# A hybrid diffusion step on one core: z/dt projection first, output projection's first columns inside the ordered region, second shift off TensorE

## The chip, the cores and the metric

The kernel runs on one core of a Trainium2 chip. The time is that of one execution on the device in microseconds (us); the figure for a kernel is the median of its runs. TensorE does matrix products and transposes, VectorE (DVE) and ScalarE (ACT) do elementwise work, GpSimd (POOL) does elementwise work and issues DMAs, and SyncE (SP) issues the large weight loads. Each engine works through one queue in a fixed order.

## The reference

One layer of a model with 128 context tokens and 256 latent tokens (384 together), width 2048, all in fp32:

```python
sh1, sc1, g1, sh2, sc2, g2 = split(silu(cond) @ w_mod + b_mod, 6)   # cond: c or c_ctx, 2 rows
h = x * (1 + sc1) + sh1
q, k, v, u, gt, z, xbc, dt = split(h @ w_in)
o_a = attention(q, k, v, cached keys and values, bias)              # 16 heads, A
o_b = silu(layer_norm(dwconv31(u * sigmoid(gt))))                   # B
xbc = silu(dwconv5(xbc)); dt = softplus(dt + dt_bias)
o_c = rms_norm((ssd_forward + ssd_backward + d * xs) * silu(z))     # C, chunks of 128
mix = concat(o_a, o_b, o_c) @ w_out                                 # 2048 x 2048
x = layer_norm(ALPHA * x + g1 * mix)
h = x * (1 + sc2) + sh2
x = layer_norm(ALPHA * x + g2 * ffn(h))                             # 5632 wide, dwconv3, SwiGLU
```

## The kernel before, in words

**Precision.** Most fp32 products are done as three passes: a matrix is split into a high part (rounded by ScalarE, line 226, tile `whi`) and a low part (the difference, by VectorE, line 227, tile `wlo`), and high x high, high x low and low x high are summed in PSUM. A weight piece of 512 KB is loaded by SyncE into one of four `raw` buffers, split as two halves, and used by TensorE; `whi` and `wlo` have eight half-piece buffers each. The products with tokens in PSUM's partitions (`tok_mm`, lines 444 to 446) have 512 columns (264 in the z/dt projection), those with channels there (`chan_mm`, lines 450 to 452) have 384.

**Stages.** First sc1, sh1, h, and the u, gt and xbc columns of `h @ w_in` with the first half of v. Then an *ordered region* (lines 871 to 890), in which TensorE's instructions stand in the order in which the program writes them: the other half of v (`phase_v`), q and k of head pair 0, the z/dt projection (`phase_zd`), q and k of pairs 1 to 7. Then the output projection (`wo`) in column groups of 512, 512, 512, 256 and 256, with gate, residual and LayerNorm statistics behind each (`mix_evac`), LayerNorm (`ln1`), and the FFN, which is the rest of the kernel.

**What sets the order around the change.** Beside the main projections a small planner (`_Flow`) keeps generators with due times: after each few matmuls `flow.tick` moves its clock on and runs what is due. The generators are: transposes of xbc (`tok_gen`), the state-space scan (`ssm_gen`, which waits for `dt_gen`), attention (`attn_gen`; pairs 5 to 7 wait until the scan is through), the LayerNorm of branch B, and `mod2_gen`, which computes g1, sc2 and sh2 with cond as a 32-column weight (line 762; 32 loads of 512 KB into three `v` buffers for each of the three, in sets of three pieces). A second list (`flow.bg`) holds the 124 taps of the 31-wide convolution for VectorE (lines 351 and 355) and hands them out at `flow.rate` of the time that ticks. When the projections are written, `flow.drain` writes whatever is left, with no projection between. Outside the region, and on all other engines everywhere, a list scheduler sets the order by its own estimate of times and by priority; weight loads and splits have a high one (`HP`).

Inside the FFN the second gate g2 is already computed without TensorE: `g2_piece` loads rows of `w_mod` into a `raw` buffer and VectorE multiplies them by cond (spread over the partitions by a DMA) and sums along the row (line 820, 128 x 512, the sum into `macc`).

The order of `wo`'s rows is `ORDER`: branch B (8 to 11), heads 0 to 3, branch C (12 to 15), heads 4 to 7.

Of the kernel before, what the change touches and what calls it, by code (L numbers as in the profile page):

```python
# [14 lines left out]
D = 2048  # L15
KC = 16
# [31 lines left out]
class _Flow:  # L48
# [29 lines left out]

    def drain(self):
        while self.bg:  # L80
            self.bg.pop(0)[0]()
        while self.q:
            self.now = max(self.now, self.q[0][0])
            self.run()
# [12 lines left out]
def _build(tc, ctx, a):  # L97
# [264 lines left out]
    def conv_ln_gen():  # L362
# [21 lines left out]
        for i in range(4):  # L384
# [5 lines left out]
            cat[8 + i] = c  # L390
        yield 2.7, 0.0
# [211 lines left out]
    def ssm_gen():  # L603
# [10 lines left out]
        ready.add("ssm")  # L614

# [116 lines left out]
    def attn_gen():  # L732
        for hp in range(8):
# [35 lines left out]
    def mod2_end(g):  # L769
# [17 lines left out]
        dst, bias = (s2, b2p) if g == 1 else (h2b, P_("bsh2", 0, 16))  # L787
        V.tensor_tensor(out=dst.rearrange("p (j b) c -> p j b c", j=4), in0=pv,
                        in1=bc(bias.rearrange("p (j b) -> p j b", j=4), 3, 2), op=ALU.add)
        yield 0.5, 1.0  # L790

    def mod2_gen(most, gap):
        i = 0
        while i < 96:
# [28 lines left out]
    def g2_piece(i):  # L823
# [47 lines left out]
    with tc.manual_schedule(engines={mybir.EngineType.PE}):  # L871
        for i in range(8):
            do_conv5(i)
        for i in range(4):
            flow.bg += conv31_steps(i)
        flow.rate = 0.4
        flow.add(30.0, tok_gen())
        flow.add(0.0, mod2_gen(3, 8.0))
        flow.add(40.0, conv_ln_gen())
# [75 lines left out]
    def mix_evac(t, cg, c0, n, ps, gb):  # L955
        rr = r[t][cg][:, c0:c0 + n]
        tmp = g_t(512)
        with tc.high_priority(offset=HP):
            V.tensor_tensor(out=tmp[:, :n], in0=ps[:, :n], in1=gb[t > 0][:, c0:c0 + n], op=ALU.mult)
        V.scalar_tensor_tensor(out=rr, in0=rr, scalar=ALPHA, in1=tmp[:, :n], op0=ALU.mult, op1=ALU.add)  # L960
        V.bn_stats(out=st1[t][:, cg + c0 // 256, :], in_=rr)

    for cg in range(4):
        gb = [gate(0, s, cg) for s in range(2)]
        for t in range(3):
            if cg % 2 == 0:
                rt[t][cg // 2] = vt_t() if cg == 0 else (ckv_t, ckv_t, v_t)[t]()
            r[t][cg] = rt[t][cg // 2][:, cg % 2, :]
            G.dma_start(out=r[t][cg], in_=a["xtok"][128 * t:128 * t + 128, 512 * cg:512 * cg + 512])
        n = 512 if cg < 3 else 256  # L970
        npk = 1024 // n
        ps = [ps_t() for _ in range(3)]
        for kk in range(KC // npk):
            hi, lo = wpiece(a["wo"][:, KC * 512 * cg + kk * 1024:KC * 512 * cg + (kk + 1) * 1024], 1024)
# [282 lines left out]
```

## Time and profile before

| what | us |
|---|---|
| median of 3 runs (lowest, highest) | 1859.7 (1859.32, 1862.12) |
| the profiled execution's own time | 1860.49 |
| its span in the trace | 1858.6 |
| TensorE busy | 1814.3 |
| VectorE busy | 1144.0 |
| ScalarE busy | 779.7 |
| GpSimd busy | 57.3 |

The profile comes from the one profiled execution, whose time is 1.9 us above its span and 0.8 us above the median. Matmuls are pipelined, so the distance from one start to the next is what one costs; the printed duration of one is longer. [...] A timeline gives instructions in order of time, with the idle time ahead of one and what ended it in brackets.

### The profile page before, as it was taken

The numbers are of one execution on the slowest core, as the hardware profiler recorded it, in microseconds if no ns is written. First come the engines' busy times: TensorE is split into PE (matmuls) and PEld (weight loads), VectorE is DVE, ScalarE is ACT, GpSimd is POOL, SyncE is SP. The second block draws the span as 40 slices with busy tenths as digits, with TensorE's granted clock in tenths as the row PEclk, the third lists the DMA queues.
The fourth block names the chain that finished last, engine by engine and source line by source line (L and its number), as shares of the span: only waits on it lengthen the run. The fifth ranks groups of instructions, "written<-read, shape, count | busy, mean of one in ns | idle before, by whom it ended". The sixth has DMA issues, their size and how long they took to land. (4 is left out here: it accounts for less than half of the span.)

```text
span 1858.6 us, 29014 instructions
## 1 busy us (share of the span) xinstructions
PE 1814.3 (98%) x11054; PEld 1634.8 (88%) x11054; DVE 1144.0 (62%) x2329; ACT 779.7 (42%) x1479; POOL 57.3 (3%) x141
## 2 busy tenths in 40 slices
PE   8999999999987999999999999999999999999998
PEld 6888978887854889999988999988999988999987
DVE  3865899457552448566733667644667644666577
ACT  4222544465555336444433444422444423444424
POOL 0000000110101000000000000000000000000000
PEclk9999999999987999999999999999999999999999
DMA  8999477776755543444444454444444444444454
GB/s 314 308 323 318 142 258 250 268 272 227 243 191 175 170 140 122 136 143 136 159 125 131 159 171 161 141 127 142 161 163 159 147 125 142 147 159 158 119 152 139
DMA packets 108011, 335.67 MB, mean 181 GB/s; under 512 B 12456, under 2 KB 17032, under 8 KB 107872
## 3 DMA queue, kind: packets, MB, share of 16 engines
q1 hardware_dynamic: 101280, 311.65, 50.9%
q0 software_dynamic: 6592, 22.18, 4.0%
q8 instruction: 86, 1.41, 0.3%
q14 instruction: 53, 0.43, 0.1%
HBM read 328.98 MB, written 4.79 MB: 180 GB/s over the span
## 5 line engine op out<-in xcount | busy, mean ns | idle before, releaser
L226 ACT CAST whi<-raw 128x512 fp32r<-128x512 f32 (+1 forms) x755 | 467.9, 621 | 908.7 <-PE mm L451 320.5
L227 DVE TENSOR_TENSOR wlo<-raw,whi 128x512 fp32r<-128x512 f32 (+1 forms) x755 | 521.1, 691 | 488.3 <-ACT whi L226 484.8
L450 PE MATMUL mm<-hl,whi 128*128 128x384 f32 x1245 | 427.0, 343 | 1.4 <-ACT whi L226 1.1
L451 PE MATMUL mm<-hl,whi 128*128 128x384 f32 x1245 | 420.1, 337 | 0.0
L452 PE MATMUL mm<-hl,wlo 128*128 128x384 f32 x1245 | 419.3, 337 | 0.0
L450 PEld LDWEIGHTS mm<-hl,whi 128*128 128x128 f32 x1245 | 233.8, 188 | 13.4 <-issue 6.7
L451 PEld LDWEIGHTS mm<-hl,whi 128*128 128x128 f32 x1245 | 234.1, 188 | 0.9 <-DVE hl L243 0.4
L452 PEld LDWEIGHTS mm<-hl,wlo 128*128 128x128 f32 x1245 | 234.0, 188 | 0.0
L450 PE MATMUL sc<-hl,whi 128*128 128x384 f32 x659 | 222.8, 338 | 0.0
L451 PE MATMUL sc<-hl,whi 128*128 128x384 f32 x659 | 221.8, 337 | 0.0
L452 PE MATMUL sc<-hl,wlo 128*128 128x384 f32 x659 | 221.7, 336 | 0.0
L450 PEld LDWEIGHTS sc<-hl,whi 128*128 128x128 f32 x659 | 123.6, 188 | 2.9 <-ACT whi L226 1.6
L451 PEld LDWEIGHTS sc<-hl,whi 128*128 128x128 f32 x659 | 123.7, 188 | 0.0
L452 PEld LDWEIGHTS sc<-hl,wlo 128*128 128x128 f32 x659 | 123.7, 188 | 0.0
L820 DVE SCALAR_TENSOR_TENSOR junk<-raw,gb 128x512 bf16<-128x512 f32 x128 | 87.9, 686 | 47.5 <-DMA raw<-wg 47.4
L444 PE MATMUL mm<-whi,hl 128*128 128x512 f32 (+2 forms) x261 | 92.5, 355 | 1.0 <-ACT m L437 0.8
L446 PE MATMUL mm<-whi,hl 128*128 128x512 f32 (+2 forms) x261 | 90.8, 348 | 0.0
L444 PE MATMUL mm<-whi,t 128*128 128x512 f32 (+1 forms) x232 | 90.6, 390 | 0.0
L445 PE MATMUL mm<-wlo,hl 128*128 128x512 f32 (+2 forms) x261 | 90.5, 347 | 0.0
L445 PE MATMUL mm<-wlo,t 128*128 128x512 f32 (+1 forms) x232 | 90.5, 390 | 0.0
L446 PE MATMUL mm<-whi,t 128*128 128x512 f32 (+1 forms) x232 | 90.4, 390 | 0.0
L355 DVE SCALAR_TENSOR_TENSOR t<-g,par,t 128x399 f32<-128x399 f32 x120 | 73.4, 630 | 1.3
(337 smaller groups left out, 2458.4 us busy)
## 6 DMA issues: line engine op xcount, KB each, us to landing
raw<-wu SPq DMA_DIRECT2D x176, 512.0 KB, 3.7
v<-wm SPq DMA_DIRECT2D x96, 512.0 KB, 5.4
raw<-wd SPq DMA_DIRECT2D x79, 512.0 KB, 3.6
m<-wm SPq DMA_DIRECT2D x128, 256.0 KB, 5.6
raw<-wA SPq DMA_DIRECT2D x32, 512.0 KB, 5.4
raw<-wqk SPq DMA_DIRECT2D x32, 512.0 KB, 4.4
raw<-wo SPq DMA_DIRECT2D x32, 512.0 KB, 3.6
raw<-wg SPq DMA_DIRECT2D x32, 512.0 KB, 3.6
```

Source lines behind the costliest of these rows:

```text
L226: S.copy(out=hi[:, :w], in_=rw)
L227: V.tensor_tensor(out=lo[:, :w], in0=rw, in1=hi[:, :w].bitcast(F32), op=ALU.subtract)
L355: V.scalar_tensor_tensor(out=cvo[i][:, :399], in0=glu[i][:, j:j + 399], scalar=P_("conv_w", 31 * i + j), in1=cvo[i][:, :399], op0=ALU.mult ...
L444: PE.matmul(ps[:, :n], A, hi[:, w0:w0 + n], start=k == 0, stop=False)
L445: PE.matmul(ps[:, :n], A, lo[:, w0:w0 + n], start=False, stop=False)
L446: PE.matmul(ps[:, :n], B, hi[:, w0:w0 + n], start=False, stop=k == last)
L450: PE.matmul(ps[:, :T], A, hh[k], start=k == k0, stop=False)
L451: PE.matmul(ps[:, :T], A, hl[k], start=False, stop=False)
L452: PE.matmul(ps[:, :T], B, hh[k], start=False, stop=k == k1)
L820: V.scalar_tensor_tensor(out=j, in0=w, scalar=1.0, in1=cbc[s], op0=ALU.mult, op1=ALU.mult, accum_out=macc[:, 16 * s + kt, kq:kq + 1])
```

## The change

1. `phase_zd` and `dt_gen` come first in the region, then `phase_v`, then q and k of all eight pairs. The taps are handed out at 0.7 in place of 0.4, `mod2_gen` has a gap of 11.5 us in place of 8.0, and the scan and attention start with due times of 30 and 50 us.
2. The first 512 columns of `wo` move into the region, behind the last q and k and ahead of the drain (`wo_group`, `cat_split`). Rows whose input isn't there yet make the planner run its generators until it is (`flow.advance`).
3. sh2 no longer goes through `mod2_gen` (64 pieces in place of 96). It is computed as g2 is, with its own array `wsh2`: odd pieces by VectorE (`dve_gemv`), even ones by a GpSimd product into an `m` tile and a ScalarE sum over it (`pool_gemv`). From the end of the scan one piece is written every 9 us; from the second group of `wo` on, one behind each weight piece.

```diff
-        while i < 96:
+        while i < 64:
...
+    def pool_gemv(w, kt, kq):
+        for s in range(2):
+            j = m_t()
+            G.tensor_tensor(out=j, in0=w, in1=cbc[s], op=ALU.mult)
+            S.activation(out=j, in_=j, func=AF.Copy, accum_out=macc[:, 16 * s + kt, kq:kq + 1])
+
+    def sh2_piece():
+        i = sh2_done[0]
+        if i == 32:
+            return
+        sh2_done[0] += 1
+        kq, pr = i // 8, i % 8
+        if pr == 0:
+            cond_rows(kq, m_t)
+        raw = load(a["wsh2"][kq, pr], 1024)
+        for e in range(2):
+            (dve_gemv if i % 2 else pool_gemv)(raw[:, 512 * e:512 * e + 512], 2 * pr + e, kq)
...
+    def wo_group(cg, ps, ready_of, after):
+        n = 512 if cg < 3 else 256
+        npk = 1024 // n
+        for kk in range(KC // npk):
+            hi, lo = wpiece(a["wo"][:, KC * 512 * cg + kk * 1024:KC * 512 * cg + (kk + 1) * 1024], 1024)
+            for k in range(npk):
+                o = npk * kk + k
+                ready_of(order[o])
+                for t in range(3):
+                    tok_mm(ps[t], ch[order[o]], cl[order[o]], t, hi, lo, n * k, n, o)
+                after(k == npk - 1)
+
+    def cat_split(k):
+        if ch[k] is not None:
+            return
+        while k not in ready:
+            flow.advance()
...
+            split(cat[k], ch[k], cl[k])
...
-        flow.rate = 0.4
+        flow.rate = 0.7
         flow.add(30.0, tok_gen())
-        flow.add(0.0, mod2_gen(3, 8.0))
+        flow.add(0.0, mod2_gen(3, 11.5))
         flow.add(40.0, conv_ln_gen())
-        flow.add(0.0, ssm_gen())
-        flow.add(0.0, attn_gen())
-        phase_v()
-        k = qk_tile(0, 0)
-        qk[0] = (qk_tile(1, 0), k)
+        flow.add(30.0, ssm_gen())
+        flow.add(50.0, attn_gen())
+        flow.add(60.0, sh2_gen(9.0))
         phase_zd()
         flow.add(0.0, dt_gen())
-        for hp in range(1, 8):
+        phase_v()
+        for hp in range(8):
             k = qk_tile(0, hp)
             qk[hp] = (qk_tile(1, hp), k)
+        ps = [mm_t() for _ in range(3)]
+        for k in ORDER[:12]:
+            cat_split(k)
+        wo_group(0, ps, cat_split, lambda last: flow.tick(2.09))
+        ready.add("stop")
         flow.drain()
...
+    for cg in range(1, 4):
+        gb = mix_rows(cg)
+        ps = [ps_t() for _ in range(3)]
+        wo_group(cg, ps, lambda k: None, lambda last: sh2_piece() if last else None)
         for t in range(3):
-            mix_evac(t, cg, 0, n, ps[t], gb)
+            mix_evac(t, cg, 0, 512 if cg < 3 else 256, ps[t], gb)
+    sh2_end()
```

The first place is TensorE's queue behind the last q and k, the *tail*. Before, it runs one attention step into the next with only sc2 and sh2 pieces (`gm<-v`) or nothing between; `at<-cons,p` are transposes of softmax rows, `at<-pt` products with values, `sc<-qk` scores:

```order
L712 MATMUL at_6174<-cons_66,p_6137 128x128 x3
L762 MATMUL gm_5496<-v_6154,cond_63 32x256 x4
L762 MATMUL gm_5496<-v_6156,cond_63 32x256 x4
L762 MATMUL gm_5496<-v_6158,cond_63 32x256 x4
L724 MATMUL at_6192<-pt_6172,ckv_2597 64x128
L724 MATMUL at_6192<-pt_6178,ckv_2597 64x128
L724 MATMUL at_6192<-pt_6172,vt_327 64x128
L724 MATMUL at_6192<-pt_6178,vt_327 64x128
L724 MATMUL at_6192<-pt_6172,vt_328 64x128
L724 MATMUL at_6192<-pt_6178,vt_328 64x128
L684 MATMUL sc_6210<-qk_5625,qk_5723 128x128
L684 MATMUL sc_6211<-qk_5625,qk_5723 128x128
```

In the change, products of `wo`'s first group (`mm<-whi,hl`) stand between the steps:

```order
L729 MATMUL at_6300<-pt_6236,ckv_3101 64x128
L448 MATMUL mm_6148<-whi_6310,hl_6161 128x512
L449 MATMUL mm_6148<-wlo_6311,hl_6161 128x512
L450 MATMUL mm_6148<-whi_6310,hl_6162 128x512
L448 MATMUL mm_6149<-whi_6310,hl_6161 128x512
L449 MATMUL mm_6149<-wlo_6311,hl_6161 128x512
L450 MATMUL mm_6149<-whi_6310,hl_6162 128x512
L448 MATMUL mm_6150<-whi_6310,hl_6161 128x512
L449 MATMUL mm_6150<-wlo_6311,hl_6161 128x512
L450 MATMUL mm_6150<-whi_6310,hl_6162 128x512
L717 MATMUL at_6327<-cons_66,p_6246 128x128 x3
L717 MATMUL at_6333<-cons_66,p_6253 128x128 x3
```

From the last q and k to the end of attention 9 or 18 such products stand between one step and the next, 141 in all.

The second place is VectorE's queue where dt is computed. Before, the taps are through for the time being and the steps of dt (`sm`, `dtv`, `dA`) stand between weight splits alone:

```order
L439 TENSOR_TENSOR dtr_88<-mm_3537,par_68 128x16
L466 SCALAR_TENSOR_TENSOR sm_3794<-dtr_88 128x48
L227 TENSOR_TENSOR wlo_3837<-raw_3830,whi_3836 128x512
L468 TENSOR_SCALAR sm_3795<-sm_3794 128x48
L469 TENSOR_SCALAR sm_3796<-sm_3795 128x48
L470 TENSOR_SCALAR sm_3797<-sm_3796 128x48
```

In the change the same steps come earlier and a tap of the 31-wide convolution (`t<-g,par,t`) stands ahead of nearly each:

```order
L358 SCALAR_TENSOR_TENSOR t_3021<-g_3015,par_68,t_3021 128x399
L479 TENSOR_TENSOR sm_3136<-sm_3136,sm_3138 128x48
L358 SCALAR_TENSOR_TENSOR t_3021<-g_3015,par_68,t_3021 128x399
L230 TENSOR_TENSOR wlo_3348<-raw_3345,whi_3347 128x512
L480 TENSOR_TENSOR sm_3136<-sm_3136,sm_3135 128x48
L358 SCALAR_TENSOR_TENSOR t_3021<-g_3015,par_68,t_3021 128x399
L481 SCALAR_TENSOR_TENSOR dtv_90<-dtr_88,sm_3136 128x48
L358 SCALAR_TENSOR_TENSOR t_3021<-g_3015,par_68,t_3021 128x399
L485 TENSOR_TENSOR dA_95<-dtv_90,sm_3151 128x48
```

Up to the last of these rows VectorE's queue of the change has, from the first weight split of the region on, 71 taps (46 of the 31-wide convolution with 399 columns, 25 of the 5-wide one with 386), 25 weight splits and 29 smaller instructions; up to the first scaling of a scan's output row (`m_3427`, 128x512, once it is divided by its norm) it has 123 taps, 47 splits and 74 others.

The third place is VectorE's queue inside a later group of `wo`. Before, weight splits stand alone there:

```order
L227 TENSOR_TENSOR wlo_7109<-raw_7106,whi_7108 128x512
L227 TENSOR_TENSOR wlo_7113<-raw_7106,whi_7112 128x512
L227 TENSOR_TENSOR wlo_7137<-raw_7134,whi_7136 128x512
L227 TENSOR_TENSOR wlo_7141<-raw_7134,whi_7140 128x512
L227 TENSOR_TENSOR wlo_7165<-raw_7162,whi_7164 128x512
```

In the change products with sums for sh2 (`junk,macc`) stand among them, four for each second weight piece, and GpSimd's queue has four products for each of the other pieces:

```order
L230 TENSOR_TENSOR wlo_7282<-raw_7279,whi_7281 128x512
L826 SCALAR_TENSOR_TENSOR junk_7309,macc_99<-raw_7307,m_7261 128x512
L230 TENSOR_TENSOR wlo_7286<-raw_7279,whi_7285 128x512
L826 SCALAR_TENSOR_TENSOR junk_7311,macc_99<-raw_7307,m_7263 128x512
L826 SCALAR_TENSOR_TENSOR junk_7313,macc_99<-raw_7307,m_7261 128x512
L230 TENSOR_TENSOR wlo_7320<-raw_7317,whi_7319 128x512
L826 SCALAR_TENSOR_TENSOR junk_7315,macc_99<-raw_7307,m_7263 128x512
L230 TENSOR_TENSOR wlo_7324<-raw_7317,whi_7323 128x512
```

Of the 32 pieces of sh2, 12 lie ahead of the second group of `wo` and 20 in the rest, 16 products on each of the two engines for a full group. On SyncE each of these loads stands between two `wo` loads and takes one of the same four `raw` buffers.

## Rows read from the trace of the kernel before

**Rows 1.** The page, part 1: busy us of each engine, share of the span, instructions

```profile
PE 1814.3 (98%) x11054; PEld 1634.8 (88%) x11054; DVE 1144.0 (62%) x2329; ACT 779.7 (42%) x1479; POOL 57.3 (3%) x141
```

**Rows 2.** Stretches: busy us of each engine (x instructions), granted clock, DMA share, GB/s

```profile
224.50:330.00 105.50, 104.51 (x791) 87.42 (x790) 98.97 (x188) 49.67 (x94) 0.56 (x1) 1.00 0.71 246
330.00:530.00 200.00, 194.97 (x1480) 166.44 (x1478) 112.42 (x234) 105.28 (x260) 24.82 (x43) 0.99 0.74 252
530.00:603.90 73.90, 54.97 (x391) 35.03 (x392) 32.44 (x86) 47.51 (x124) 6.59 (x13) 0.79 0.50 164
603.90:694.50 90.60, 90.60 (x392) 73.42 (x393) 41.52 (x64) 27.44 (x45) 5.13 (x10) 1.00 0.52 156
```

**Rows 3.** TensorE's waits from 530 to 604: us in total, times, longest

```profile
PE at L712 <- ACT p L702: 8.5, 7, 2.1
PE at L595 <- DVE m L591: 6.6, 1, 6.6
PE gm L762 <- DMA v<-wm: 2.7, 3, 1.3
```

**Rows 4.** Timeline of TensorE, one attention step in the tail: start, us, instruction

```profile
579.77 0.39 PE L689 MATMUL sc<-ckv,qk 64*128 64x128 f32 x4
...
582.80 0.55 PE L712 MATMUL at<-cons,p 128*128 128x128 f32 x3 [0.59 <-ACT p L702]
```

**Rows 5.** Timeline of TensorE, a set of three modulation pieces and the closing transposes

```profile
503.49 1.50 PE L762 MATMUL gm<-v,cond 128*32 128x256 f32 x24
504.92 0.49 PE L566 MATMUL at<-t,t 128*128 128x128 f32 x2
...
584.13 0.64 PE L785 MATMUL at<-cons,gb 128*128 128x128 f32 x4
```

**Rows 6.** Timeline of TensorE, z/dt products of 264 columns and `wo` products of 512

```profile
301.59 0.28 PE L446 MATMUL mm<-whi,hl 128*128 128x264 f32 x1
...
302.20 0.28 PE L445 MATMUL mm<-wlo,hl 128*128 128x264 f32 x1
...
606.21 0.39 PE L444 MATMUL mm<-whi,hl 128*128 128x512 f32 x1
606.44 0.39 PE L445 MATMUL mm<-wlo,hl 128*128 128x512 f32 x1
```

**Rows 7.** Timeline of VectorE, the region's first weight split, then splits and taps

```profile
219.14 0.69 DVE L227 TENSOR_TENSOR wlo<-raw,whi 128x512 fp32r<-128x512 f32 x1
...
264.97 0.68 DVE L227 TENSOR_TENSOR wlo<-raw,whi 128x512 fp32r<-128x512 f32 x1
265.57 3.35 DVE L355 SCALAR_TENSOR_TENSOR t<-g,par,t 128x399 f32<-128x399 f32 x6
```

**Rows 8.** Stretches around a short stop of TensorE

```profile
420.00:430.00 10.00, 7.96 (x48) 7.17 (x47) 3.84 (x7) 4.73 (x16) 2.55 (x5) 1.00 0.64 214
430.00:440.00 10.00, 10.00 (x69) 7.77 (x70) 8.59 (x21) 7.39 (x21) 0.73 (x2) 0.83 0.63 199
```

**Rows 9.** A full group of `wo` as a stretch

```profile
661.00:694.50 33.50, 33.50 (x147) 27.12 (x146) 16.53 (x27) 9.93 (x16) 1.07 (x2) 1.00 0.49 143
```

**Rows 10.** Groups by line: busy us, mean ns of one, idle before

```profile
L820 DVE SCALAR_TENSOR_TENSOR junk<-raw,gb 128x512 bf16<-128x512 f32 x128 | 87.9, 686 | 47.5 <-DMA raw<-wg 47.4
...
L550 POOL TENSOR_SCALAR_AFFINE_SELECT m<-m 128x512 f32<-128x512 f32 x12 | 8.3, 702 | 21.7 <-DMA m<-csd 21.5
L588 ACT ACTIVATE m<-m 128x512 f32<-128x512 f32 x3 | 1.9, 632 | 5.0 <-DVE m L585 4.9
```

**Rows 11.** Timelines of VectorE and GpSimd where both work on 128x512 tiles

```profile
479.86 1.86 DVE L583 TENSOR_TENSOR m<-m,m 128x512 f32<-128x512 f32 x1
481.75 1.00 DVE L585 TENSOR_TENSOR m<-m,m 128x512 f32<-128x512 f32 x1
...
369.20 1.60 DVE L227 TENSOR_TENSOR wlo<-raw,whi 128x512 fp32r<-128x512 f32 x1 [0.85 <-ACT whi L226]
...
479.93 2.27 POOL L550 TENSOR_SCALAR_AFFINE_SELECT m<-m 128x512 f32<-128x512 f32 x3
```

More of the change, by code (lines that the diff above doesn't have):

```diff
@@ L77, in tick, with advance @@
             self.run()
+    def advance(self):
+        self.now = max(self.now, self.q[0][0])
+        self.run()
     def drain(self):
@@ L82, in drain @@
         while self.q:
-            self.now = max(self.now, self.q[0][0])
-            self.run()
+            self.advance()
 class _Halves:
@@ L390, in conv_ln_gen @@
             cat[8 + i] = c
+            ready.add(8 + i)
         yield 2.7, 0.0
@@ L614, in ssm_gen @@
         ready.add("ssm")
+        ready.update(range(12, 16))
     vt = [None] * 3
@@ L829, in g2_piece, with sh2_gen, sh2_end @@
             dve_gemv(raw[:, 512 * e:512 * e + 512], 2 * pr + e, kq)
+    sh2_done = [0]
+    def pool_gemv(w, kt, kq):
[14 more added lines that the diff above has]
+            (dve_gemv if i % 2 else pool_gemv)(raw[:, 512 * e:512 * e + 512], 2 * pr + e, kq)
+    def sh2_gen(gap):
+        while "ssm" not in ready:
+            yield 0.0, 1.0
+        while "stop" not in ready:
+            sh2_piece()
+            yield 0.0, gap
+    def sh2_end():
+        m = s_t(32)
+        V.tensor_reduce(out=m, in_=macc, axis=AX.X, op=ALU.add)
+        V.tensor_tensor(out=h2b.rearrange("p k s -> p s k"), in0=m.rearrange("p (s k) -> p s k", s=2),
+                        in1=bc(P_("bsh2", 0, 16), 1, 2), op=ALU.add)
     def g2_end():
@@ L908, in gate, with mix_evac, mix_rows @@
         return t
+    def mix_evac(t, cg, c0, n, ps, gb):
+        rr = r[t][cg][:, c0:c0 + n]
+        tmp = g_t(512)
+        with tc.high_priority(offset=HP):
+            V.tensor_tensor(out=tmp[:, :n], in0=ps[:, :n], in1=gb[t > 0][:, c0:c0 + n], op=ALU.mult)
+        V.scalar_tensor_tensor(out=rr, in0=rr, scalar=ALPHA, in1=tmp[:, :n], op0=ALU.mult, op1=ALU.add)
+        V.bn_stats(out=st1[t][:, cg + c0 // 256, :], in_=rr)
+    def mix_rows(cg):
+        for t in range(3):
+            if cg % 2 == 0:
+                rt[t][cg // 2] = vt_t() if cg == 0 else (ckv_t, ckv_t, v_t)[t]()
+            r[t][cg] = rt[t][cg // 2][:, cg % 2, :]
+            G.dma_start(out=r[t][cg], in_=a["xtok"][128 * t:128 * t + 128, 512 * cg:512 * cg + 512])
+        return [gate(0, s, cg) for s in range(2)]
@@ new lines, in wo_group @@
+    def wo_group(cg, ps, ready_of, after):
[6 more added lines that the diff above has]
+                ready_of(order[o])
+                for t in range(3):
+                    tok_mm(ps[t], ch[order[o]], cl[order[o]], t, hi, lo, n * k, n, o)
+                after(k == npk - 1)
@@ L954, in _build @@
     h2g = [None] * 4
[L955 to L964, printed above, removed]
-        for t in range(3):
[L966 to L974, printed above, removed]
-            for k in range(npk):
-                o = npk * kk + k
-                for t in range(3):
-                    tok_mm(ps[t], ch[order[o]], cl[order[o]], t, hi, lo, n * k, n, o)
-        for t in range(3):
-            mix_evac(t, cg, 0, n, ps[t], gb)
+    for cg in range(1, 4):
+        gb = mix_rows(cg)
+        ps = [ps_t() for _ in range(3)]
+        wo_group(cg, ps, lambda k: None, lambda last: sh2_piece() if last else None)
+        for t in range(3):
+            mix_evac(t, cg, 0, 512 if cg < 3 else 256, ps[t], gb)
+    sh2_end()
     LW = 256
```

54 lines of the change are left out of this document (29 added, 25 removed).

## The prediction

> **What bounds the kernel now.** I read the page first: TensorE is busy for 1814.3 of 1858.6 us [rows 1], so what the change is worth is TensorE's time: work taken off it, its stops, and its clock. Next I cut the ordered region and the first three groups of `wo` into stretches [rows 2], 470.0 us from the region's first matmul at 224.5 to the last 512-column product at 694.5. The reader is to subtract TensorE's busy time from the length: it stops for 1.0, 5.0, 18.9 and 0.0 us. [...] The waits there [rows 3] are softmax rows from ScalarE (8.5), the scan's last output row from VectorE (6.6), and modulation loads (2.7). One attention step shows why [rows 4]: from the last score product at 579.77 to the first transpose at 582.80 the chain over VectorE and ScalarE takes 3.0 us, and what TensorE has beside it is too short.
>
> **The change, part by part.** I work from the profiled execution, 1860.5 us.
>
> *sh2 leaves TensorE.* [...] That is -15.9 us. It holds whole only because TensorE bounds the stretches. The pieces that lie in the tail's waits did cover some of them; those waits are in the next term.
>
> *The tail gets cover.* The scan now ends well before the last q and k, so the 6.6 us wait on its last row goes. Between attention steps stand 9 or 18 products of 0.23 us [rows 6], 2.1 or 4.1 us, against the 3.0 us that the chain takes; scores have 18 behind them, and then value products too. What is late next is the very end: behind the last head come a copy and a split of its output before its `wo` rows can be used, and for that I leave 2.5 us. Of 18.9 us of stops 16.4 go. With TensorE busy the clock should stay at 1.00, as it does in all the stretches where it doesn't stop [rows 2]; I leave 0.5 of the 11.5. Together -27.4 us. The bounds are 0, if attention remains the limit, and -30.4.
>
> *VectorE in the first 120 us of the region.* Before, VectorE is already busy for 98.97 of 105.5 us there [rows 2]; its order gives weight splits precedence and taps the rest, and TensorE hardly waits. Now the taps come at 0.7 instead of 0.4, and dt, whose steps stood behind the taps, stands among them. From the region's first split, at 219.14, to dA the queue holds 71 taps at 3.35 / 6 = 0.56, 25 splits at 0.60 [rows 7], and 29 smaller instructions that I put at half a tap: 39.8 + 15.0 + 8.1 = 62.9 us, so dA is there at 282.0. TensorE reaches the product with dA behind 288 products of 264 columns at 0.122, 45 of 512 at 0.23 [rows 6], three sets of modulation pieces and 18 transposes at 0.16 [rows 5]: 35.1 + 10.4 + 4.3 + 2.9 = 52.7 us from 224.5, at 277.2. It will stand 4.8 us there, with all of v behind it in its queue. The density goes on (52 taps and 22 splits more up to the scan's first output row), so it is not won back and may grow; I take 6 us. A stop costs clock behind it: 2.0 us of stops from 420 to 430 were followed by a clock of 0.83 over ten busy us, 1.7 us [rows 8]; I add 2. So +8 us, between 0 (the scheduler's slack is larger than it looks) and about 20 (the same again at the scan's products, with the clock).
>
> *sh2 on VectorE, GpSimd and ScalarE.* A full group of `wo` takes 33.5 us, in which VectorE is busy 16.5 and ScalarE 9.9 [rows 9]. VectorE gets 16 products of 0.686 [rows 10], 11.0 us; 6.0 us stay free. ScalarE gets 16 sums like the one at 0.632 [rows 10], 10.1 us, and has 23 free. The DMAs get another 512 KB for each weight piece (18 products of 0.23, 4.2 us), 125 GB/s more than the 143 [rows 9], and 246 to 252 were kept up earlier [rows 2]: not the limit. These run beside TensorE and cost nothing as long as the splits come in time. What the trace of before does not show is a GpSimd product of two tiles. Its one-input select over 128x512 takes 0.70 on average [rows 10], and reading two tiles one after the other would make it 1.40. More important is what it does to VectorE: while three selects ran on GpSimd from 479.93 for 2.27 us, two VectorE instructions that read two SBUF tiles took 1.86 and 1.00 us, and a split at 369.20 took 1.60 [rows 11]; alone such an instruction takes 0.69 [rows 7]. The first two lost 1.48 us to 2.27 us of GpSimd work, 0.65 us for each; all three lost 2.4 to the 8.3 us that all 12 selects took [rows 10], 0.29 for each. A group has 16 GpSimd products, 11.2 to 22.4 us; VectorE would lose 3.2 to 14.6 us of its 6.0 free ones, so the group is 0 to 8.6 us longer, and in two and a half groups that is 0 to 21 us. If VectorE lost all of GpSimd's time, it would be up to 16.4 a group, 41 us. I take 2 us a group, 5 in all, near the lower rate, since the splits are made some pieces ahead. The 12 pieces in the region come every 9 us or slower and are covered by attention's gaps on VectorE.
>
> [...]
>
> *Order of loads and queues.* The `raw` ring of four now serves two streams, so a `wo` load can stand in SyncE's queue behind a sh2 load that waits for GpSimd to give up a buffer, and gate and residual loads stand in GpSimd's queue behind products. With `whi` and `wlo` holding four pieces I count this as nothing; gone, it costs what the products cost beyond 8.4 us for a pair of pieces. The larger gap of `mod2_gen` only spreads the sets.
>
> *Sum.* -15.9 - 27.4 + 8 + 5 = -30.3 us: 1860.5 - 30.3 = 1830.2. The median lies 0.8 below the profiled execution, so 1829.4; I say 1830.
>
> **Rivals.** (a) *VectorE's taps hold the region up for longer*: the 8 us become 20 to 25 because the scan's products wait in the same queue and the clock falls again. For it: 98.97 of 105.5 us busy already. Against: the splits have precedence, and the wait before was 1 us. About 1845.
> (b) *The tail stays attention's*: the planner's order covers the chain on paper, but ScalarE, which now also sums sh2 in order and stands still when GpSimd is late, delays the softmax, and half of the 27.4 us stays. For it: ScalarE is busy 47.5 of 73.9 us in the tail [rows 2]. Against: mid-region steps with the same spacing hardly wait. 1830 + 14 = 1844.
> (c) *GpSimd's products block VectorE whole, and it gets slower than before.* Place: `wo`'s second to fourth group; TensorE waits for `wlo`. Each product takes x us off VectorE, a group grows by 16x - 6.0, and the rest of the change is worth 35.3 us, so it decides from x = 1.26 us on. At x = 1.40 the 5 us become 41: 1829.4 + 36 = 1865; at 1.6, 1874. For it: a split that took 1.60. Against: 0.29 to 0.65 is what the selects took.
> (d) *It works better than I charge*: no lateness of VectorE and no loss in `wo`, 1829.4 - 13 = 1816.
> That it doesn't do what it says can be left out: the queues show the pieces gone from TensorE and the products between the steps.
>
> **How the numbers follow.** Forecast 0.52 (own range 1821 to 1839), (a) 0.14, (b) 0.13, (c) 0.10, (d) 0.11. The range for 8 in 10 leaves out (c), most of (d)'s lower half and the upper edge of (a) and (b): 1814 to 1853. A measurement of this kernel can tell about 0.2%, 3.7 us, from no change. Forecast, (a), (b) and (d) are below 1856, but for a few parts in 100 that (a) or (b) run on to there; of (c) most is above 1863.4: faster 0.86, same 0.05, slower 0.09.
>
> **What would show it.** In the profile after, TensorE's stretch up to the last 512-column product should be some 30 us shorter than 470; modulation pieces should be 64, not 96 (512 records of line 762's successor in place of 768); the last q and k should be followed by `wo` products at a clock of 1.00, and the waits on softmax rows be under 3 us. A wait of 4 to 7 us on dt's or the scan's VectorE steps should stand some 55 us into the region, with a lower clock behind it. VectorE's splits in `wo` should sometimes take over 1 us, always beside a GpSimd product, and TensorE should wait for `wlo` there for no more than some 5 us in total. It is wrong if that wait is over 20 us (c), if TensorE stops for 10 us or more behind the last q and k (b), or if it stops for over 15 us before 400 (a).

## The result, and the profile after

| | median us | lowest, highest | runs |
|---|---|---|---|
| before, beside it | 1859.51 | 1859.14, 1862.12 | 4 |
| changed | 1890.97 | 1888.23, 1892.16 | 4 |

The ratio is 1.0164 (95% interval 1.0146 to 1.0182): 31.5 us slower, where 30 us faster was forecast. Line numbers of the changed kernel are 3 to 7 higher than those of before up to `mod2_end`: `wlo` is written on line 230, `whi` on 229; 448 to 450 are the `wo` products, 842 GpSimd's product, 843 ScalarE's sum, 826 VectorE's product.

Part 1 of the page of the changed kernel, which answers to [rows 1]:

```profile
PE 1811.3 (96%) x10794; PEld 1635.4 (87%) x10794; DVE 1186.7 (63%) x2457; ACT 816.1 (43%) x1606; POOL 148.9 (8%) x213
```

By the forecast's count TensorE has 15.9 us less to do, but it is busy for only 3.0 us less. The stretches of the changed kernel show where, with the columns of [rows 2]; the region starts at 224.98, its last q and k end at 565.80, the last 512-column product at 710.50, and the first 384-column product of the up-projection starts at 776.10:

```profile
224.98:330.00 105.02, 100.75 (x713) 86.72 (x716) 102.81 (x201) 48.17 (x91) 7.80 (x13) 0.98 0.66 226
330.00:480.00 150.00, 138.12 (x1007) 116.15 (x999) 94.11 (x193) 89.00 (x221) 23.42 (x34) 0.97 0.59 195
480.00:565.80 85.80, 73.97 (x496) 64.12 (x493) 41.05 (x108) 54.54 (x150) 23.25 (x22) 0.90 0.68 230
565.80:628.00 62.20, 53.50 (x299) 38.40 (x298) 28.07 (x70) 34.36 (x91) 24.17 (x27) 0.92 0.58 187
628.00:710.50 82.50, 72.86 (x290) 55.70 (x290) 54.10 (x105) 34.05 (x78) 39.49 (x35) 0.96 0.68 218
710.50:776.10 65.60, 54.46 (x433) 52.24 (x432) 51.72 (x118) 39.97 (x98) 12.26 (x12) 0.97 0.40 135
```

The reader subtracts again: TensorE stops for 4.3, 11.9, 11.8, 8.7, 9.6 and 11.1 us, 57.5 in all, and no stretch has a granted clock of 1.00, a share of TensorE's full speed. What a lower one means is seen behind the stop at 416 to 419 us: from 422 to 424 us the clock is 0.50, and products of 384 columns start 0.32 us apart; from 426 to 430, at 1.00, some 0.18. The region up to the last 512-column product takes 485.5 us against 470.0, and from there to the up-projection's first 384-column product 65.6 against 53.6 before. Behind that the kernels run alike: the whole stretch is 27.5 us longer, the span 27.9 (the profiled execution of the changed kernel is the fastest of its four). TensorE's waits in the changed kernel, 225 to 777 us (us in total, times, longest), answer to [rows 3]:

```profile
PE at L717 <- ACT p L707: 19.5, 10, 4.7
PE mm L448 <- DVE g L925: 4.8, 1, 4.8
PE at L717 <- ACT t L733: 4.8, 2, 2.6
PE sc L448 <- DVE g L925: 3.6, 1, 3.6
PE at L492 <- issue: 3.4, 1, 3.4
...
PE mm L448 <- ACT whi L229: 2.7, 2, 1.5
...
PE mm L449 <- DVE wlo L230: 2.3, 4, 1.6
```

No single wait is large, and the tail of [rows 3] has not gone but spread. The softmax waits grew from 8.5 to 19.5 us; not all of that is sh2's, since the changed kernel without sh2 (below) has 11.2. New are two waits for PSUM banks that VectorE empties late (`g`, line 925). How one of them comes about is seen in the queues of the second `wo` group. SyncE's loads (start, us), then GpSimd, ScalarE, VectorE and TensorE:

```profile
646.55 0.33 SPq L216 DMA_DIRECT2D raw<-wo  x1
647.29 0.33 SPq L216 DMA_DIRECT2D raw<-wsh  x1
...
656.61 0.33 SPq L216 DMA_DIRECT2D raw<-wo  x1
657.36 0.33 SPq L216 DMA_DIRECT2D raw<-wsh  x1
```

```profile
641.47 5.05 POOL L842 TENSOR_TENSOR m<-raw,m 128x512 f32<-128x512 f32 x4 [7.01 <-DMA raw<-wsh]
651.54 5.04 POOL L842 TENSOR_TENSOR m<-raw,m 128x512 f32<-128x512 f32 x4 [5.01 <-DMA raw<-wsh]
661.51 5.11 POOL L842 TENSOR_TENSOR m<-raw,m 128x512 f32<-128x512 f32 x4 [4.93 <-DMA raw<-wsh]
```

```profile
645.93 0.61 ACT L229 CAST whi<-raw 128x512 fp32r<-128x512 f32 x1
646.56 0.63 ACT L843 ACTIVATE m<-m 128x512 f32<-128x512 f32 x1
...
647.19 1.12 ACT L229 CAST whi<-raw 128x512 fp32r<-128x512 f32 x2
...
652.87 0.63 ACT L843 ACTIVATE m<-m 128x512 f32<-128x512 f32 x1 [1.99 <-POOL m L842]
```

```profile
666.68 0.69 DVE L230 TENSOR_TENSOR wlo<-raw,whi 128x512 fp32r<-128x512 f32 x1 [4.95 <-ACT whi L229]
...
667.90 0.69 DVE L925 TENSOR_TENSOR g<-sc,gb 128x512 f32<-128x512 f32 x1
```

```profile
668.64 0.80 PE L448 MATMUL sc<-whi,hl 128*128 128x512 f32 x1 [3.56 <-DVE g L925]
```

Four products end at 646.52. At 646.55 SyncE issues the `wo` load that had waited for their `raw` buffer, behind it at 647.29 the next sh2 load, which lands 4.2 us later; at 651.54 GpSimd goes on. One turn takes 10.0 us and serves two weight pieces; TensorE needs 8.4 us for them (33.5 us for eight [rows 9]). From 641.47 to 719.84 GpSimd makes seven turns, 11.2 us each on average. In the same turn casts of `wo` weights stand behind sums that wait for GpSimd (53.8 us of such waits over the run). Two turns on, VectorE stands 4.95 us in order for such a cast, the instruction that empties a PSUM bank stands behind it, and TensorE, which needs the bank, stops for 3.6 us.

### The profile page after: what moved, and what is told of

Read it like the earlier page. It is cut to its first block, busy times and chain, and to the rows that moved or that the text cites. A ratio compares the mean times of both kernels' runs of the same rounds, so it can differ in the third digit from the quotient of the medians.

```text
span 1886.5 us, 28860 instructions
## 1 busy us (share of the span) xinstructions
PE 1811.3 (96%) x10794; PEld 1635.4 (87%) x10794; DVE 1186.7 (63%) x2457; ACT 816.1 (43%) x1606; POOL 148.9 (8%) x213
## 3 DMA queue, kind: packets, MB, share of 16 engines
q8 instruction: 84, 1.38, 0.3%
## 5 line engine op out<-in xcount | busy, mean ns | idle before, releaser
L230 DVE TENSOR_TENSOR wlo<-raw,whi 128x512 fp32r<-128x512 f32 (+1 forms) x755 | 528.0, 701 | 483.2 <-ACT whi L229 476.1
L454 PEld LDWEIGHTS mm<-hl,whi 128*128 128x128 f32 x1245 | 236.0, 190 | 11.9 <-issue 5.7
L448 PE MATMUL mm<-whi,hl 128*128 128x512 f32 (+2 forms) x293 | 104.1, 355 | 7.7 <-DVE g L925 4.8
L449 PE MATMUL mm<-wlo,hl 128*128 128x512 f32 (+2 forms) x293 | 101.8, 347 | 2.3 <-DVE wlo L230 2.3
L450 PE MATMUL mm<-whi,hl 128*128 128x512 f32 (+2 forms) x293 | 101.3, 346 | 0.0
L842 POOL TENSOR_TENSOR m<-raw,m 128x512 f32<-128x512 f32 x64 | 86.7, 1383 | 117.9 <-DMA raw<-wsh 94.4
```

What stands on the lines that cost most here:

```text
L230: V.tensor_tensor(out=lo[:, :w], in0=rw, in1=hi[:, :w].bitcast(F32), op=ALU.subtract)
L448: PE.matmul(ps[:, :n], A, hi[:, w0:w0 + n], start=k == 0, stop=False)
L449: PE.matmul(ps[:, :n], A, lo[:, w0:w0 + n], start=False, stop=False)
L450: PE.matmul(ps[:, :n], B, hi[:, w0:w0 + n], start=False, stop=k == last)
L454: PE.matmul(ps[:, :T], A, hh[k], start=k == k0, stop=False)
L842: G.tensor_tensor(out=j, in0=w, in1=cbc[s], op=ALU.mult)
```

## The experiments

Where the time of a kernel lies is read from TensorE's timeline in three stretches: from the first product of the region to the end of the last q and k (R), from there to the end of the last 512-column product of `wo` (W), and from there to the up-projection's first 384-column product (L). Each kernel ran beside before, whose median was 1859.1 to 1860.6.

| kernel | median us | ratio to before, interval | R | W | L |
|---|---|---|---|---|---|
| changed | 1891.0 | 1.0164 (1.0146, 1.0182) | 340.8 | 144.7 | 65.6 |
| sh2_left_out | 1832.4 | 0.9862 (0.9846, 0.9879) | 325.3 | 115.3 | 53.5 |
| sh2_tensor | 1845.5 | 0.9932 (0.9916, 0.9947) | 334.4 | 119.4 | 53.5 |
| sh2_vector | 1858.0 | 0.9992 (0.9980, 1.0003) | 331.7 | 122.8 | 66.3 |
| sums_later | 1901.6 | 1.0231 (1.0215, 1.0247) | 337.5 | 152.2 | 76.6 |
| loads_only | 1840.2 | 0.9895 (0.9881, 0.9910) | 330.0 | 121.5 | 53.5 |
| own_buffers | 1895.2 | 1.0198 (1.0179, 1.0216) | 353.7 | 147.8 | 53.4 |
| own_vector | 1845.4 | 0.9925 (0.9910, 0.9940) | 338.2 | 115.3 | 53.5 |
| own_at_place | 1889.8 | 1.0162 (1.0144, 1.0180) | 340.4 | 150.3 | 60.2 |
| own_sums_later | 1880.6 | 1.0115 (1.0097, 1.0132) | 331.7 | 145.9 | 61.6 |
| gpsimd_ahead | 1874.6 | 1.0077 (1.0060, 1.0094) | 335.3 | 146.5 | 53.5 |
| gpsimd_ahead_9 | 1880.3 | 1.0108 (1.0093, 1.0123) | 329.8 | 144.7 | 67.1 |
| vector_ahead | 1831.9 | 0.9851 (0.9836, 0.9866) | 326.7 | 115.4 | 53.5 |
| vector_ahead_silu | 1835.2 | 0.9866 (0.9852, 0.9881) | 328.2 | 115.2 | 53.5 |
| contention_only | 1884.6 | 1.0132 (1.0117, 1.0147) | 345.3 | 147.5 | 53.5 |
| gpsimd_half_no_sums | 1866.2 | 1.0043 (1.0029, 1.0058) | 328.8 | 130.3 | 71.3 |
| gpsimd_half_sums | 1874.7 | 1.0085 (1.0070, 1.0100) | 330.0 | 145.6 | 60.1 |
| vector_half | 1837.6 | 0.9891 (0.9874, 0.9907) | 326.6 | 116.7 | 57.8 |

**What the new path costs, and what the rest of the change is worth.** Four kernels from the changed one. *Pinned* means that an instruction is kept behind what is written so far on its engine; without that, the order on every engine but TensorE is set when the program is built.

```diff
 sh2_left_out:  - flow.add(60.0, sh2_gen(9.0))      and no sh2_piece() in wo_group
 sh2_tensor:    + 32 more pieces in mod2_gen, with the gap of 8.0 of before;
                no sh2_gen, no sh2_piece()
 sh2_vector:    - (dve_gemv if i % 2 else pool_gemv)(raw...)
                + dve_gemv(raw...)
 sums_later:    pool_gemv appends its tile to pend; S.activation(...) over pend comes
                at the next GpSimd piece, pinned behind what ScalarE has by then
```

> The changed kernel with sh2's weights neither loaded nor multiplied (sh2 is its bias alone): the price of the new path by difference. A and B: 1891 - 37 = 1854, between 1846 and 1862. C: 1884 to 1891. The forecast of before had 5 us for this path in wo, which would be 1886.

> The changed kernel's region order and its first wo group inside the region, but sh2 is made on TensorE again in 32 modulation pieces (about 15.9 us of TensorE). A and B both say that the 29 us of stops behind sums and weights and their 8 us of clock go: 1891 - 37 + 16 = 1870, between 1862 and 1878. C: the stops stay and the pieces come on top, or cover a few of them: 1891 to 1907.

> The changed kernel (1891.0 us), but all 32 sh2 pieces take VectorE's path; GpSimd has no products and ScalarE no sums of them. Theory A (order chain: GpSimd's product takes 1.38 us on average, the sums stand in ScalarE's queue and wait 53.8 us for it, and softmax rows and weight casts stand behind them): of TensorE's 57.5 us of stops between 225 and 776 us, 29 stand behind such sums or weights, with some 8 us of clock; they go, but VectorE gets 20 x 2.74 = 55 us in the last three wo groups where 27 stood, beside 27 of its own in 82.5 us, so it is about full there: 1868, between 1860 and 1878. Rival B (the loads: a second stream through the ring of four raw buffers): the loads are the same, 1885 to 1891. Rival C (the region's new order alone, without sh2: the taps' rate, zd first, wo's first group and its 12 splits): 1882 to 1891.

> The changed kernel, but ScalarE's sums of GpSimd's products are held back until the next GpSimd piece is issued and pinned there in ScalarE's order, some 8 us later in wo and 18 us in the region: the same products, loads and sums, another place. A, if the wait in ScalarE's order is the price: 25 of the 37 us go, 1866, between 1858 and 1875. A, if it is ScalarE's time or GpSimd's contention with VectorE: 1886 to 1893. B: the raw buffers are given up as late as before, 1885 to 1893. C: 1886 to 1893.

Without sh2 the kernel takes 1832.4: the new path costs 58.6 us, far more than A or B allowed, and the rest of the change is worth 27.4. With sh2 back on TensorE the change is a gain, 14 us. So the region's order (rival C) is out. Its stretches without sh2 show no stop and a clock of 1.00 where the tail was:

```profile
225.00:330.00 105.00, 101.04 (x717) 86.85 (x719) 102.77 (x201) 48.12 (x91) 7.80 (x13) 0.98 0.66 226
330.00:480.00 150.00, 138.11 (x1010) 116.23 (x1001) 92.85 (x197) 92.50 (x227) 15.85 (x28) 0.98 0.59 195
480.00:550.30 70.30, 66.39 (x485) 57.75 (x485) 29.10 (x73) 40.97 (x109) 2.14 (x4) 0.98 0.61 205
550.30:665.60 115.30, 115.30 (x588) 90.19 (x588) 52.73 (x99) 45.44 (x94) 10.65 (x20) 1.00 0.54 165
```

With GpSimd's half given to VectorE (`sh2_vector`) the kernel takes 1858.0, 33 us less than the changed one and 2 below A's range. Theory A fell in `sums_later`: ScalarE waited for GpSimd's products no more, and the kernel got 10.6 us slower. The wait had gone elsewhere. GpSimd, SyncE and VectorE of that kernel:

```profile
604.42 5.91 POOL L849 TENSOR_TENSOR m<-raw,m 128x512 f32<-128x512 f32 x4 [13.97 <-DMA raw<-wsh]
```

```profile
610.36 0.33 SPq L216 DMA_DIRECT2D raw<-wsh  x1
```

```profile
614.47 0.69 DVE L826 SCALAR_TENSOR_TENSOR junk<-raw,m 128x512 bf16<-128x512 f32 x1 [6.51 <-DMA raw<-wsh]
...
617.03 0.56 DVE L700 CUSTOM_DVE_ANT_0 sc<-sc,gb 128x384 f32<-128x384 f32 x1
```

SyncE can load sh2 at 610.36 only, when GpSimd has given up a buffer at 610.33; VectorE stands 6.5 us at its product, in order, with a softmax step behind it.

**Is it the shared ring of four `raw` buffers?** The first two load sh2 into `m` tiles.

```diff
-        raw = load(a["wsh2"][kq, pr], 1024)
+        raw = [load(a["wsh2"][kq, pr][:, 512 * e:512 * e + 512], 512, m_t()) for e in range(2)]
 own_vector: the same, and dve_gemv for every piece
 loads_only: load() through raw, then only V.tensor_copy(out=s_t(1), in_=raw[:, 0:1])
 before_new_sh2: the kernel before, mod2_gen with 64 pieces and a gap of 11.5, sh2_piece() behind each
                 weight piece of wo's four groups, the rest of the 32 in front of sh2_end()
```

> The changed kernel with the same GpSimd and VectorE products and the same sums, but sh2's weights are loaded in two halves into m tiles (13 in that ring) instead of the raw ring of four that wo's weights use. Theory B' (the loop through the raw ring: in wo a wo load waits until GpSimd's four products, 5.05 us, give up a raw buffer, sh2's next load stands behind it in SyncE's queue and takes 4.2 us, and GpSimd waits 5.0 us for it: 10.05 us for two weight pieces in place of TensorE's 8.4): the 33 us between the changed kernel and the one with all sh2 on VectorE go, and part of the 25.6 us beyond: 1891 - 40 = 1851, between 1842 and 1860. Rival A' (GpSimd's 1.38 us a product and ScalarE's sums themselves, by contention or by ScalarE's time): 1880 to 1893.

> The kernel with all sh2 on VectorE (1858.0 us), its weights in m tiles. B': the two streams no longer share four buffers, the loads run ahead and VectorE takes its products where it is idle, before the last wo groups: 1840, between 1834 and 1847. Rival: VectorE's 88 us of products are the price wherever they stand: 1854 to 1860.

> The changed kernel with sh2's weights loaded through the raw ring as there, but not multiplied (one column of each is copied, so a buffer is given up on landing; sh2 is its bias alone). The kernel without these loads takes 1832.4 us. B': a buffer is held for the load's 4.2 us alone, 1834 to 1840. Rival D (the loads' bytes, 512 KB a piece, are the price whatever reads them): 1845 to 1858.

> The kernel before with only sh2 moved: 28 of its 32 pieces in the four wo groups, alternately on GpSimd with ScalarE and on VectorE, through the raw ring; the region's order and the place of wo's first group are those of before. B': 15.9 us of TensorE go, 14 pairs of weight pieces take 10.05 us in place of 8.4, 23 us, and some 8 us of clock: 1875, between 1865 and 1885. Rival C' (the price arises only with the changed kernel's order, where attention and wo stand beside each other): 1844 to 1852.

For VectorE's path the ring was worth 12.6 us (1858.0 to 1845.4), and the loads alone cost 7.8; but with GpSimd nothing is gained (1895.2), against B'. L falls from 65.6 to 53.4, so the loop is gone there, while R grows by 13: sh2's pieces, no longer held back by the ring, run beside the attention. What they do there is seen on VectorE, with GpSimd's products behind it:

```profile
634.61 6.14 DVE L230 TENSOR_TENSOR wlo<-raw,whi 128x512 fp32r<-128x512 f32 x1
...
644.26 5.58 DVE L230 TENSOR_TENSOR wlo<-raw,whi 128x512 fp32r<-128x512 f32 x1 [0.66 <-ACT whi L229]
```

```profile
635.20 5.00 POOL L842 TENSOR_TENSOR m<-m,m 128x512 f32<-128x512 f32 x4
...
644.36 4.92 POOL L842 TENSOR_TENSOR m<-m,m 128x512 f32<-128x512 f32 x4
```

A split of 0.69 us takes 6.14 and 5.58, each time for as long as four products run. `before_new_sh2` took 1910.3, ratio 1.0272 (1.0255, 1.0290), 25 us above the highest that B' allowed: the path is dear in the old order too, against C'.

**Loop, order or contention?** Each takes one of them away.

```diff
 own_at_place:      own_buffers, with each sh2 load pinned at its place in SyncE's queue
 own_sums_later:    own_at_place, with the pinned later sums of sums_later
 vector_ahead:      own_vector, loads one piece ahead of the products, products pinned,
                    sh2_gen(3.5) in place of sh2_gen(9.0)
 vector_ahead_silu: vector_ahead, the eight SiLUs of conv_ln_gen in a later step, pinned
```

> Own m buffers for sh2's weights as in own_buffers (1895.2 us), but each sh2 load is pinned in SyncE's queue where the program has it, so that the pieces stay where the changed kernel has them: 12 in the region, 20 in wo. Theory B' (the loop through the raw ring is the price in wo): in wo the loop goes, lastqk to last wo product falls from 144.7 to some 125 us and the stretch behind from 65.6 to 54, and the region keeps its waits: 1891 - 20 - 12 = 1859, between 1848 and 1868. Rival E (GpSimd's products slow VectorE's own instructions from 0.69 to 1.7 us and more, wherever the weights lie): 1885 to 1900.

> own_at_place with ScalarE's sums held back by one GpSimd piece and pinned. If, with the loop gone, sums that wait for GpSimd in front of softmax rows are the rest of the price: 10 to 15 us below own_at_place, 1846 by the figure expected there. If GpSimd's contention with VectorE is: the same as own_at_place within 4 us. If buffers held longer delay GpSimd: above it.

> All sh2 on VectorE with own buffers (own_vector 1845.4 us), but each piece's weights are loaded one piece ahead of its products, the products are pinned in VectorE's order, and the region takes a piece every 3.5 us in place of 9. In own_vector VectorE stood 4.3 us in order for sh2's weights with softmax steps behind it. If such waits are the rest (13 us above the kernel without sh2): 1836, between 1829 and 1841. If VectorE's time or the bytes are: 1843 to 1850.

> vector_ahead, and the convolution branch's eight SiLUs on ScalarE (3.6 us and a table load) are put into a step of their own 7 us later and pinned, so that they don't stand in front of a softmax row; TensorE stopped 7.1 us behind them at 416 us in every kernel with the changed order. If that is their price with the clock: 6 to 9 us below vector_ahead, 1829. If the next softmax row meets them instead: the same within 3 us.

Own buffers with the loads kept in their places change nothing (1889.8): the loop closes through ScalarE, since `wo`'s buffers are given up by casts and splits that stand behind the sums. GpSimd's turns in `wo`, from 643.5 to 664.4 us there, are still 10.3 and 10.6 us long, and this is what ScalarE waits for it from 565 to 720 us (in total, times, longest):

```profile
ACT m L843 <- POOL m L842: 53.2, 34, 5.7
```

Later sums on top give 9 us. With all of sh2 on VectorE, loaded a piece ahead, pinned and with a piece every 3.5 us (three edits beyond `own_vector`, not told apart), the path costs nothing that can be measured: 1831.9, 0.5 us from the kernel without it, and 1.5% faster than before. VectorE carries its 128 products where it had been idle; the stretches of `vector_ahead` from 480 to the last 512-column product:

```profile
480.00:549.90 69.90, 65.98 (x484) 57.65 (x483) 58.79 (x172) 40.21 (x106) 4.30 (x8) 0.98 0.95 339
549.90:665.30 115.40, 115.39 (x589) 90.33 (x588) 100.58 (x259) 46.08 (x95) 11.78 (x22) 1.00 0.73 242
```

Moving the SiLUs did not help (1835.2): the waits for softmax rows fell from 11.2 to 6.5 us, but those for the scan's copies behind them rose from 1.1 to 5.9.

```diff
 gpsimd_ahead:    vector_ahead, every second piece as GpSimd products (pinned) and ScalarE
                  sums (pinned at the next GpSimd piece)
 gpsimd_ahead_9:  the same with sh2_gen(9.0)
 contention_only: vector_ahead
+        if pr % 2 == 0:
+            for e in range(4):
+                tc.keep_in_program_order(G.tensor_tensor(out=m_t(), in0=rows[0], in1=rows[1], op=ALU.mult))
```

> vector_ahead (1831.9 us) with every second piece on GpSimd and ScalarE as in the changed kernel: 64 products on GpSimd, loads one piece ahead, products pinned, sums held back to the next GpSimd piece and pinned. F (late data at the head of in-order queues is the price): no loop is left, VectorE loses a few us: 1836, between 1830 and 1845. E (GpSimd's products slow VectorE, whatever stands where): 1860 to 1885.

> The same with a piece every 9 us in the region, as in the changed kernel, so that 20 of 32 pieces stand in the last three wo groups. F: 1840, between 1832 and 1850. E: 1865 to 1890.

> vector_ahead with 64 products on GpSimd beside it that nothing waits for: two rows of the condition multiplied into an m tile that nobody reads, four for every second piece, pinned at its place; VectorE still makes all of sh2. E: VectorE, fuller than in the changed kernel, loses 40 us or more: 1860 to 1885. F: VectorE loses 5 to 15 us, part of them idle time: 1834 to 1845.

E is right here and F wrong: with loads a piece ahead and the sums a GpSimd piece later the GpSimd half still costs 42.7 us against `vector_ahead` (48.4 with a piece every 9 us), and 64 products whose results nobody reads cost 52.6. Loads do wait there for `m` buffers that these products hold (SyncE 48.7 us, from 470 to 720), but the data come in time: VectorE waits 0.2 us for sh2's weights and ScalarE 2.5 for `wo`'s. VectorE of `contention_only` beside GpSimd:

```profile
582.21 1.33 DVE L856 SCALAR_TENSOR_TENSOR junk<-m,m 128x512 bf16<-128x512 f32 x1
583.47 1.75 DVE L230 TENSOR_TENSOR wlo<-raw,whi 128x512 fp32r<-128x512 f32 x1
585.14 1.77 DVE L856 SCALAR_TENSOR_TENSOR junk<-m,m 128x512 bf16<-128x512 f32 x1
586.96 1.65 DVE L856 SCALAR_TENSOR_TENSOR junk<-m,m 128x512 bf16<-128x512 f32 x1
588.55 0.68 DVE L230 TENSOR_TENSOR wlo<-raw,whi 128x512 fp32r<-128x512 f32 x1
```

```profile
581.66 6.41 POOL L851 TENSOR_TENSOR m<-m,m 128x512 f32<-128x512 f32 x4
```

While four products run on GpSimd, VectorE gets through four instructions: one for one. By group, 470 to 720 us (busy us, mean ns of one), first `contention_only`, then `vector_ahead`:

```profile
L856 DVE SCALAR_TENSOR_TENSOR junk<-m,m 128x512 bf16<-128x512 f32 x128 | 127.2, 993 | 1.9 <-DMA m<-wsh 0.2
L230 DVE TENSOR_TENSOR wlo<-raw,whi 128x512 fp32r<-128x512 f32 x72 | 61.1, 850 | 14.1 <-ACT whi L229 14.0
```

```profile
L853 DVE SCALAR_TENSOR_TENSOR junk<-m,m 128x512 bf16<-128x512 f32 x128 | 88.0, 687 | 3.2 <-DMA m<-wsh 1.5
L230 DVE TENSOR_TENSOR wlo<-raw,whi 128x512 fp32r<-128x512 f32 x84 | 57.6, 688 | 18.5 <-ACT whi L229 18.2
```

VectorE's products took 39.2 us more and its splits 72 x 0.162 = 11.7: 50.9 us for the 100.4 us that GpSimd was busy with its products, 0.51 for each.

**The halves of the changed kernel by themselves.**

```diff
 gpsimd_half_no_sums: pieces with i % 2 == 1 left out, S.activation of pool_gemv left out
 gpsimd_half_sums:    pieces with i % 2 == 1 left out
 vector_half:         pieces with i % 2 == 0 left out
```

> The changed kernel with the 16 GpSimd pieces alone (loads through the raw ring and 64 products; VectorE's 16 pieces and ScalarE's sums are left out, so sh2 is its bias). Without all of sh2 it takes 1832.4 us; 32 loads alone cost 7.8. E (contention with VectorE, which is half empty here): VectorE loses 12 to 25 us, part of it idle time: 1845 to 1858. F (the loops need ScalarE's sums in front of the casts): 1836 to 1844.

> The same with ScalarE's 64 sums of these products, where the scheduler puts them (sh2 is still its bias). F: the sums put the casts behind GpSimd, and the loop of 10 us for 8.4 closes: 20 to 35 us above the kernel without sums, 1860 to 1878. E: ScalarE has room, within 5 us of the kernel without sums.

> The changed kernel with VectorE's 16 pieces alone (GpSimd's 16 and the sums left out, sh2 is its bias). All 32 on VectorE through the raw ring cost 25.6 us above 1832.4. E and F: no GpSimd, VectorE has room: 1834 to 1842. Rival: VectorE's products in order in front of the splits cost by themselves: 1845 or more.

From 1832.4 VectorE's half costs 5.1 us, GpSimd's products with their loads 33.8, ScalarE's sums of them 8.5 more. The sums thus cost less than F's 20 to 35 and more than E's 5. Both halves together cost 58.6, 11.2 above the sum of the parts. Without any sums the loop closes all the same. SyncE, then GpSimd, of `gpsimd_half_no_sums`:

```profile
637.07 0.38 SPq L216 DMA_DIRECT2D raw<-wsh  x1
637.55 10.36 SPq L216 DMA_DIRECT2D raw<-wo  x2
648.00 0.38 SPq L216 DMA_DIRECT2D raw<-wsh  x1
```

```profile
641.66 5.89 POOL L842 TENSOR_TENSOR m<-raw,m 128x512 f32<-128x512 f32 x4 [5.03 <-DMA raw<-wsh]
652.64 6.39 POOL L842 TENSOR_TENSOR m<-raw,m 128x512 f32<-128x512 f32 x4 [5.09 <-DMA raw<-wsh]
```

The second of the two `wo` loads at 637.55 is issued 10 us later, when the products end at 647.55, and sh2's load behind it at 648.00: a turn of 11.0 us for 8.4, 1 us longer than in the changed kernel, since four products take 5.9 to 6.4 us here. F's claim that the loop needs the sums is wrong, and so is E's figure, which had no loop in it.

## Why the prediction was wrong

**sh2 off TensorE, -15.9.** Right in kind: 512 records of line 769 are left of 768, and the kernel with sh2 on TensorE takes 13.1 us more than the one without (1845.5 and 1832.4). The term is an estimate from [rows 5]: 1.43 us for a set of three pieces, 15.3 for 32, and 0.64 for the closing transposes.

**The tail gets cover, -27.4.** Right in mechanism: without sh2's path TensorE is busy for all 115.30 us from the last q and k on, at 1.00. The 11.5 us of clock in this term are an estimate from [rows 2], 0.21 of 54.97 busy us at a clock of 0.79, and with 18.9 us of stops they make the bound of 30.4; no run shows the clock's part by itself. In the changed kernel it stops there for 8.7 and 9.6 us; the bound given for rival (b), 10 us, is passed, and part of it by (b)'s mechanism, ScalarE's sums in front of softmax rows. The other two signs of being wrong did not come: before 400 us TensorE stops for 8.8 us, not 15 (a), and its waits for `wlo` are 2.5 us in all, not 20 (c).

**VectorE in the first 120 us, +8.** The stop at dA came where it was put, 3.4 us long at 281 against 4.8 at 277, but the loss behind it was another: at 416 and 419 TensorE stops for 7.1 us, and about there in every kernel with the new order but `sh2_tensor` (5.7) and `vector_ahead_silu`, since ScalarE's eight SiLUs of branch B (line 391) now stand in front of a softmax row:

```profile
412.65 3.61 ACT L391 ACTIVATE t<-t,par 128x128 f32<-128x128 f32 x8
416.17 0.39 ACT L707 ACTIVATE p<-p,sm 128x128 f32<-128x128 f32 x1
```

These three terms make -35.3, 1824; the kernel without sh2 took 1832.4. The missing 8 us are of the size of this stop with the clock behind it, but that is not shown: moving the SiLUs gave nothing back.

**sh2 on VectorE, GpSimd and ScalarE, +5: the step that failed.** It cost 58.6 us. The products' length was bounded rightly (1.29 in the middle, 1.38 on average and 1.26 at the shortest, of 0.70 to 1.40). VectorE's loss was a small part of the price in the changed kernel: in 628 to 710.5 its splits took 0.767 in place of 0.69, its products 0.740, and it was busy for 54.1 of 82.5 us. What failed are two terms put at nothing.

The first is the sentence on loads and queues, "I count this as nothing; gone, it costs what the products cost beyond 8.4 us for a pair of pieces". The products of a pair are 5.05 us and were compared with 8.4. But the next load can't start before they end, so the turn is products plus load plus queue, 5.05 + 4.2 + 0.75 = 10.0. From 628 to 710.5 us 290 products took 82.5 us, where 0.23 each would make 66.7: 15.8 us more. With the softmax rows and PSUM banks that come late and the lower clock (TensorE busy for 126.4 us in W, 115.3 without sh2), W grows by 29.4 and L by 12.1. That the turn is what W pays for is read from these rows; no edit that opened it gave the time back, for what came in its place is the contention below.

The second is the 12 pieces in the region, "covered by attention's gaps on VectorE". R grows by 15.5, all of it behind 480 us: there TensorE stops for 11.8 us in place of 3.9, and the clock is 0.90 in place of 0.98. In ScalarE's queue, among the softmax steps, sums wait 13.9 us for GpSimd from 330 to 566 us.

**Rival (c)** named the place, GpSimd's products in `wo`, and a slower kernel, with 0.10. Its mechanism, VectorE blocked, is a small part of what `wo`'s rows of the changed kernel show (one wait of TensorE, 1.6 us at 691, stands behind a split of 1.74); it is what comes when the loop is opened. The two stand in for each other: in 470 to 725 us a split takes 0.80 on average in the changed kernel, and 0.94 in `own_buffers`, where GpSimd waits less for its loads. No edit that kept GpSimd's products came below 1866, not even with half of the path left out. The rates taken from the selects, 0.29 to 0.65 [rows 11], held 0.51; the choice near the lower one would have been too low, had VectorE been the limit. In `own_buffers` a VectorE split lasts through four GpSimd products (6.14 and 5.58 us beside 5.00 and 4.92); in `contention_only`, from 583.47 us on, the rows show turns, one for one, at 1.65 to 1.77 us.

**What stays open.** The experiments show that GpSimd's products are what makes the path dear. How the 33.8 us that they cost alone, and the 58.6 of the whole path, divide between the loop and the contention was not told apart: each edit that removed one let the other grow.

**A version that beats both** is `vector_ahead`, with all of sh2 on VectorE, from buffers of its own, loaded a piece ahead: 1831.9 us, 0.9851 of before (0.9836 to 0.9866).

## What to carry to other kernels

An added stream that shares buffers or an in-order queue is priced by its round trip, load, queue and use together (10.0 us here), against the period of the stream beside it (8.4), and not by busy time. Before the sum is made, follow one buffer from being given up to being full again. An idle GpSimd was no free place for products of two tiles beside a VectorE that also reads two: 64 of them, read by nobody, cost 52.6 us (`contention_only`). Idle time of VectorE itself, with the load a piece ahead, was free: 1831.9 us with all of sh2 (`vector_ahead`), 1832.4 without it.

## What the runs showed of the hardware that was not expected

- Beside GpSimd products of two 128 x 512 tiles, VectorE instructions with two SBUF inputs often go one for one with them, at 1.6 to 1.8 us in place of 0.69 (`contention_only`), or one of them lasts through four products, 5.6 to 6.1 us (`own_buffers`). GpSimd loses too: in `contention_only` a product takes 1.25 us at best and 1.58 on average. VectorE's softmax step on line 700, whose first input is in PSUM, took 0.57 on average over 16 of them from 470 to 720 us there, as in `vector_ahead`; in the changed kernel it took 0.56 to 0.60 in the four cases in which it ran beside such products, and in the twelve others.
- sh2's 32 loads and 88 us of VectorE products cost nothing measurable in `vector_ahead`: the DMA engines are busy for 0.95 of their time from 480 to 550 us, and TensorE for 115.39 of the 115.40 us behind that, at 1.00.
